# Splitting and enlarging the fill of the first four steps of a chunked scan's software pipeline

## The chip, the cores and the metric

One core of a Trainium2 chip runs the whole program. The metric is the device time of one execution in microseconds (us), as the median of several runs. Engines: PE is TensorE (matmul), PEld its weight loads, DVE VectorE, ACT ScalarE, POOL GpSimd, SP SyncE, which issues nearly all DMAs here. DVE, ACT, POOL and SP each work through their own instructions in the written order, and so does PE; they wait for each other by semaphores.

## The reference, cut to what matters

One layer of a hybrid block over 1024 latent tokens (and 256 context tokens), model width 1024, float32. An input projection `u = h @ w_in` feeds a bidirectional Mamba-2 scan (8 groups of 4 heads, head dimension 64, state 128, chunks of 128 tokens), an FNet-style Fourier branch and gates; both branches are merged, then a SwiGLU FFN and a final norm follow. The part that matters is the scan:

```
states   = einsum('bcsgn,bcsgj,bcsgjp->bcgjpn', bc, decay_to_end, xdt)
entering = scan(carry * dec + st)                      # over the chunks, each direction
cb       = einsum('bclgn,bcsgn->bcgls', cc, bc)
y_diag   = einsum('bcgjls,bcsgjp->bclgjp', cb * lmat, xdt)
y_off    = einsum('bclgn,bcgjpn,bclgj->bclgjp', cc, entering, exp(a_cum))
y        = (y_diag + y_off + xs * d_skip) * silu(z)    # then a grouped RMSNorm
```

`z` and the Fourier branch's input are column blocks of the same projection `u`; they need nothing of the scan.

## The kernel before, in words

Every projection is done in float32 by three matmuls per product: weights and activations are each split into a rounded high part and the rest, and `mm3` (lines 203 to 205) multiplies high by high, high by low, low by high into one PSUM tile.

The scan stage loops over 64 steps (`nticks`), group by group, 8 chunks of 128 tokens in each group. Step n writes, in this order: `y_b` and `y_b2` of chunk n-1; `y_a` of chunk n; the DMAs for chunk n+1 (`y_load`, whose tile `abc` has two buffers); one or two state products of the next group (`state_b`); `y_c` of chunk n-4; and then some **fill**. A Python generator `fill_stream` hands out the fill one unit at a time, and `run_fill(k)` writes units until k have been written in all. So the fill is matmul work without ties to the scan, put between the scan's short dependent products so that PE has something to do.

By names: `cb` (line 908), `yo` (910 and 911), `yd` (943), `st` (881 and 882) and `ytr` (968) are the scan's own products on PE. Their followers are `cp` (917), `G` (920), `cd` (924), `dg` (925), `y` (929), `yz` (951 and 952), the state update `S` (891) and the state weights `xwf` (873) on DVE; the eight `abc` activations (915), their Exp (918) and squares and scales (953, 961) on ACT; and `xd` (932 to 935) on POOL. `cb`, `yo`, `yd` and `st` have one PSUM buffer each.

A fill unit is one output tile of 128 tokens by 256 columns: eight times `mm3`, 24 matmuls, into a PSUM tile `fill` of three buffers (`tm_units`). Eight units share one pair of weight tiles, which two ACT casts `whi` (198) and two POOL subtractions `wlo` (199) split. Units are of two kinds. A **z unit** is turned into silu(z) by an activation (802) and a DVE step (803) into a tile `zs`, of which there are 12 buffers; `y_b2` of the same group and chunk (line 952) is the last reader and sets the buffer free. A **u unit** is copied by ACT to `ust` (807, two buffers) and stored by a DMA (808); it needs no `zs` buffer. In the stream, units 0 to 15 are z units (groups 0 and 1), 16 to 23 u units, 24 to 39 z, 40 to 47 u, 48 to 63 z, 64 to 71 u, 72 to 79 z, 80 to 87 u and 88 to 95 z. Then 20 gate units follow, in the last steps and behind the loop.

The order written here is not yet the order on the engines. Pools and a list scheduler of the tile layer place each instruction when its operands and buffers are free by that scheduler's own model; a unit written before its `zs` buffer is free stands later on PE.

Of the kernel before, what the change touches and what calls it, by code (L numbers as in the profile page):

```python
# [20 lines left out]
NT = L // P  # L21
# [114 lines left out]
def build(nc, tc, h, o, hook=None, stop=None):  # L136
    es = ExitStack()
    with es:
        _build(nc, tc, h, o, hook, stop, es)


def _build(nc, tc, h, o, hook, stop, es):
# [638 lines left out]
    NPRE = 96 + 4 * sum(GSCHED)  # L781
    RT = 1
    ZSB, FOFF = 12, 4
# [212 lines left out]
    def run_fill(n):  # L996
        while nfill[0] < n:
            nfill[0] += 1
            try:
                next(fill)  # L1000
            except StopIteration:
                return
# [11 lines left out]
    nticks = NG * NT  # L1014
    groups[0].y_load(0)
    for n in range(nticks + LAG + 1):
        g, c = divmod(n, NT)
        if n < nticks:
            if c == 0 and g + 1 < NG:
                groups[g + 1] = Group(g + 1)  # L1020
                groups[g + 1].load_states()
                groups[g + 1].state_a(0)
        if n >= 1 and n - 1 < nticks:
            groups[(n - 1) // NT].y_b((n - 1) % NT)
            groups[(n - 1) // NT].y_b2((n - 1) % NT)
        if n < nticks:
            groups[g].y_a(c)
            if n + 1 < nticks:
                groups[(n + 1) // NT].y_load((n + 1) % NT)
            if g + 1 < NG:  # L1030
                for i in ((c,) if c < 7 else (7, 8)):
                    if i + 1 < 9:
                        groups[g + 1].state_a(i + 1)
                    groups[g + 1].state_b(i)
        if n >= LAG and n - LAG < nticks:
            groups[(n - LAG) // NT].y_c((n - LAG) % NT)
        if n < nticks - NT:
            run_fill(8 + FOFF + ((NPRE - 8 - FOFF) * (n + 1)) // (nticks - NT))
        else:
            run_fill(NPRE + int(RT * (n - 55)))  # L1040
    run_fill(10 ** 6)
# [667 lines left out]
```

## Time and profile before

| | |
|---|---|
| median of 3 runs | 2231.84 us (2231.05 to 2234.35) |
| the profiled execution's own time | 2232.41 us |
| its span, first to last instruction | 2230.6 us |
| mean granted clock of TensorE | 0.994 |
| PE busy in the span | 2157.4 us, 97% |
| stage of the z and u units (612.2 to 1091.0) | 478.8 us, PE busy 462.0 |
| gate units behind it (1091.0 to 1165.0) | 74.0 us, PE busy 73.5 |

The profile lists busy time by engine, what ended each idle time, and the chain that ended last; the trace gives the same for any stretch or tile.

### The profile page before, as it was taken

To read this page: it belongs to the slowest core of one execution; us is meant where nothing else is said; L and a number is where in the kernel's file an instruction comes from. 1 tells how busy PE (TensorE), PEld (TensorE's weight loads), DVE (VectorE), ACT (ScalarE), POOL (GpSimd) and SP (SyncE) were. 2 spreads that over 40 slices of the span, in tenths; PEclk is the share of its full clock that TensorE was granted. 3 is DMA by queue.
4 is the path that set the end of the run, shared out by engine and by line. 5 is a ranking of instruction groups with operands and counts; after the bars stand their busy time and mean duration, and the time that the engine had idled before them with its cause. 6 is when DMAs were issued, how large, how long until landed. Compare 5 with 4: busy or idle time off the path is not lost.

```text
span 2230.6 us, 32729 instructions
## 1 busy us (share of the span) xinstructions
PE 2157.4 (97%) x11560; PEld 1805.8 (81%) x11560; DVE 1628.0 (73%) x2795; ACT 996.0 (45%) x2093; POOL 701.7 (31%) x581
## 2 busy tenths in 40 slices
PE   6999999999999999999999999999899999999997
PEld 1778888887798999999889887877687888878876
DVE  5888888998758777877726657946987667774577
ACT  4444444445436667666743222224532333234443
POOL 1532111010125555555521221111243333332222
PEclk9999999999999999999999999999999999999999
DMA  8212223342454555555454556752476244457765
GB/s 285 77 62 95 76 89 129 126 131 99 149 172 151 175 159 173 175 167 175 151 174 177 178 172 226 246 174 81 155 267 238 86 141 145 144 201 232 235 206 179
DMA packets 167388, 360.80 MB, mean 162 GB/s; under 512 B 17580, under 2 KB 57260, under 8 KB 166584
## 3 DMA queue, kind: packets, MB, share of 16 engines
q1 hardware_dynamic: 167224, 358.71, 47.9%
q8 instruction: 91, 1.49, 0.3%
q14 instruction: 73, 0.60, 0.1%
HBM read 267.86 MB, written 90.78 MB: 161 GB/s over the span
## 4 chain that ended last, share of the span: by engine, by line
PE 74%; DVE 10%; DMA 7%; ACT 4%; issue 3%; POOL 1%; SPq 0%; DVEq 0%; POOLq 0%; ACTq 0%
PE mm L496 16%; PE dm L210 8%; PE fp L204 6%; PE fp L205 6%; PE fp L203 5%; DMA abc<-s_a 3%; PE mm L498 3%; PE spq L210 2%; PE fq L204 2%; PE fq L205 2%; ACT abc L915 2%; PE fq L203 2%; PE fill L210 2%; PE fill L203 2%; PE fill L204 2%
## 5 line engine op out<-in xcount | busy, mean ns | idle before, releaser
L199 POOL TENSOR_TENSOR wlo<-wraw,whi 128x1024 fp32r<-128x1024 f32 x80 | 198.2, 2481 | 581.3 <-ACT whi L198 515.2
L198 ACT CAST whi<-wraw 128x1024 fp32r<-128x1024 f32 x123 | 127.8, 1044 | 218.0 <-PE dm L210 79.3
L203 PE MATMUL fill<-whi,hhi 128*128 128x256 f32 x768 | 222.3, 290 | 0.6 <-ACT whi L198 0.4
L433 DVE SCALAR_TENSOR_TENSOR cv<-pad,vecs,cv 128x1282 f32<-128x1282 f32 (+1 forms) x128 | 211.1, 1679 | 9.4 <-ACT cv L430 8.8
L204 PE MATMUL fill<-wlo,hhi 128*128 128x256 f32 x768 | 216.0, 281 | 0.2 <-POOL wlo L199 0.2
L205 PE MATMUL fill<-whi,hlo 128*128 128x256 f32 x768 | 216.0, 282 | 0.0
L915 ACT ACTIVATE abc<-abc,a_all 128x128 f32<-128x128 f32 x512 | 157.7, 389 | 90.7 <-DMA abc<-s_a 86.7
L205 PE MATMUL fp<-m,opl 128*128 128x512 f32 x452 | 179.7, 398 | 4.3 <-DVE opl L1389 4.1
L203 PE MATMUL fp<-m,oph 128*128 128x512 f32 x452 | 179.7, 398 | 2.1 <-ACT m L1432 0.9
L204 PE MATMUL fp<-m,oph 128*128 128x512 f32 x452 | 179.8, 398 | 1.8 <-DVE m L1433 1.7
L496 PE MATMUL mm<-tq,whi 128*128 128x512 f32 x480 | 155.9, 405 | 2.3 <-ACT whi L198 2.3
L203 PEld LDWEIGHTS fill<-whi,hhi 128*128 128x128 f32 x768 | 144.1, 188 | 3.0 <-ACT whi L198 0.5
L204 PEld LDWEIGHTS fill<-wlo,hhi 128*128 128x128 f32 x768 | 144.6, 188 | 1.4 <-POOL wlo L199 0.6
L205 PEld LDWEIGHTS fill<-whi,hlo 128*128 128x128 f32 x768 | 144.3, 188 | 0.5
L496 PE MATMUL mm<-hhi,whi 128*128 128x512 f32 x320 | 127.5, 399 | 3.4 <-DVE pad L572 3.4
L496 PE MATMUL mm<-hlo,whi 128*128 128x512 f32 x320 | 127.6, 399 | 0.0
L496 PE MATMUL mm<-hhi,wlo 128*128 128x512 f32 x320 | 127.3, 399 | 0.0
L917 DVE COPY_PREDICATED abc<-misc,abc 128x512 f32<-128x512 int32 x64 | 52.0, 813 | 83.4 <-ACT abc L915 83.3
L496 PEld LDWEIGHTS mm<-tq,whi 128*128 128x128 f32 x480 | 91.2, 192 | 24.1 <-ACT whi L198 3.3
L205 PEld LDWEIGHTS fp<-m,opl 128*128 128x128 f32 x452 | 85.2, 189 | 26.5 <-DVE opl L1389 5.6
L891 DVE SCALAR_TENSOR_TENSOR S<-S,ead,st 128x64 f32<-128x64 f32 x512 | 104.8, 272 | 0.0
L203 PEld LDWEIGHTS fp<-m,oph 128*128 128x128 f32 x452 | 85.3, 189 | 24.0 <-ACT m L1432 1.3
(412 smaller groups left out, 5888.7 us busy)
## 6 DMA issues: line engine op xcount, KB each, us to landing
abc<-s_a SPq DMA_DIRECT2D x64, 512.0 KB
fraw<-in_wfi SPq DMA_DIRECT2D x44, 512.0 KB
wraw<-in_wxbc SPq DMA_DIRECT2D x32, 512.0 KB
dx<-in_wada SPq DMA_DIRECT2D x32, 512.0 KB
wraw<-in_wzf SPq DMA_DIRECT2D x24, 512.0 KB
gt<-s_gate SPq DMA_DIRECT2D x24, 512.0 KB
fi<-in_wfo SPq DMA_DIRECT2D x22, 512.0 KB
s_cw<-fo SPq DMA_DIRECT2D x44, 256.0 KB
```

Source lines behind the costliest of these rows:

```text
L198: nc.scalar.copy(out=hi[:, :cols], in_=raw[:, :cols])
L199: (eng or nc.gpsimd).tensor_tensor(out=lo[:, :cols], in0=raw[:, :cols], in1=hi[:, :cols].bitcast(F32), op=ALU.subtract)
L203: nc.tensor.matmul(ps, lhsT=a[0], rhs=b[0], start=start, stop=False)
L204: nc.tensor.matmul(ps, lhsT=a[0], rhs=b[1], start=False, stop=False)
L205: nc.tensor.matmul(ps, lhsT=a[1], rhs=b[0], start=False, stop=stop)
L210: nc.tensor.matmul(ps, lhsT=a[i], rhs=b[j], start=start and (i, j) == (0, 0), stop=stop and (i, j) == (1, 0))
L433: nc.vector.scalar_tensor_tensor(out=v[:, :n], in0=pd[:, t:t + n], scalar=cwh[:, 5 * b + t:5 * b + t + 1], in1=v[:, :n], op0=ALU.mult, op1 ...
L496: nc.tensor.matmul(ps, lhsT=lhs[x], rhs=b[i][y], start=i == 0 and (x, y) == (0, 0), stop=i == 3 and (x, y) == (1, 0))
L498: nc.tensor.matmul(cps, lhsT=lhs[x], rhs=(hc_hi, hc_lo)[y][c0 + i], start=first and i == 0 and (x, y) == (0, 0), stop=last and i == 3 and ...
L891: nc.vector.scalar_tensor_tensor(out=sn[:, hd_], in0=S[-1][:, hd_], scalar=decp[:, i, d, 4 * g + j:4 * g + j + 1], in1=sv_[:, hd_], op0=AL ...
L915: nc.scalar.activation(out=abc[:, d, j, :], in_=abc[:, d, j, :], func=AF.Identity, scale=-1.0, bias=a_all[:, c, hd:hd + 1])
L917: nc.vector.copy_predicated(out=E, mask=tri_b.bitcast(mybir.dt.int32)[:, None, :].to_broadcast([P, HPG, P]), data=abc[:, 1])
```

## The change

The fill of steps 0 to 3 is written in two parts. A first part stands ahead of `y_a`, up to 10, 13, 16 and 19 units in all; the second stands where it did, up to 12, 15 and 18. From step 3 on, the count rises evenly from 22 to 96 at step 55. Before, it rose evenly from 13 at step 0 to 96 at step 55. So after step 0 there is one unit less, after step 1 as many, after step 2 two more, after steps 3 to 5 four more, and the lead runs out towards step 55. No instruction is added or taken away.

```
         if n >= 1 and n - 1 < nticks:
             groups[(n - 1) // NT].y_b((n - 1) % NT)
             groups[(n - 1) // NT].y_b2((n - 1) % NT)
+        if n < 4:
+            run_fill(10 + 3 * n)
         if n < nticks:
             groups[g].y_a(c)
...
         if n < nticks - NT:
-            run_fill(8 + FOFF + ((NPRE - 8 - FOFF) * (n + 1)) // (nticks - NT))
+            run_fill(12 + 3 * n if n < 3 else 21 + ((NPRE - 21) * (n - 2)) // (nticks - NT - 3))
```

What the scheduler makes of it on the engines is shown at three places. The first is PE between the `yo` products of chunk 4 and `yd` of chunk 3, with the first three of the 24 matmuls of unit 16. Before:

```order
L908 MATMUL cb<-cT,bT 128x128
L910 MATMUL yo<-S_5151,cT 128x256
L911 MATMUL yo<-S_5111,cT 128x256
L881 MATMUL st<-xwf,bh 128x256
L882 MATMUL st<-xwb,bh 128x256
L203 MATMUL fill<-whi,hhi_190 128x256
```

and with the change:

```order
L910 MATMUL yo<-S_5151,cT 128x256
L911 MATMUL yo<-S_5111,cT 128x256
L203 MATMUL fill<-whi,hhi_190 128x256
L204 MATMUL fill<-wlo,hhi_190 128x256
L205 MATMUL fill<-whi,hlo_198 128x256
```

All 24 matmuls of unit 16 now stand ahead of the state product `st`, where they stood behind it.

The second place is ACT in the steps that follow, where the u units are copied out. Before, copies of u units alternate with the scan's activations:

```order
L807 COPY ust<-fill 128x256
L971 ACTIVATE yst<-ytr,vecs 128x128 x2
L953 ACTIVATE xd,ssq<-yz 128x256
L918 ACTIVATE abc<-abc 128x512
L807 COPY ust<-fill 128x256 x2
L953 ACTIVATE xd,ssq<-yz 128x256
L971 ACTIVATE yst<-ytr,vecs 128x128 x2
```

and with the change:

```order
L807 COPY ust<-fill 128x256
L915 ACTIVATE abc<-abc,a_all 128x128 x8
L961 ACTIVATE yz<-yz,grs 128x256 x2
L807 COPY ust<-fill 128x256
L918 ACTIVATE abc<-abc 128x512
L807 COPY ust<-fill 128x256 x4
L971 ACTIVATE yst<-ytr,vecs 128x128 x2
```

Four copies now stand in a row: on PE, units 17 to 22 are written with only one `st` between them, ahead of `yd` of chunk 4. Before, `yd` of chunk 4 stood behind unit 18.

The third place is PE around chunks 12 and 13 with the change, from the last matmul of unit 33 to what stands right ahead of unit 34:

```order
L205 MATMUL fill<-whi,hlo_205 128x256
L908 MATMUL cb<-cT,bT 128x128
L943 MATMUL yd<-xh,G 128x64 x4
L910 MATMUL yo<-S_6265,cT 128x256
L911 MATMUL yo<-S_5897,cT 128x256
L968 MATMUL ytr<-misc,yz 128x128 x2
L881 MATMUL st<-xwf,bh 128x256
L882 MATMUL st<-xwb,bh 128x256
L908 MATMUL cb<-cT,bT 128x128
L943 MATMUL yd<-xh,G 128x64 x4
L910 MATMUL yo<-S_6359,cT 128x256
L911 MATMUL yo<-S_5741,cT 128x256
```

Two `yd` and two `cb` stand here with no fill between them; before, there were one and a half units between the same two `yd`. From here to the start of unit 41, PE has seven units (34 to 40) for eight `yd` (of chunks 12 to 19; the first one shown is chunk 12's), and then units 41 to 45 in a row. Such a stretch comes again between units 62 and 65, with two units (63 and 64) for four steps.

## Rows read from the trace of the kernel before

**Rows 1.** The page: the span and the busy time of PE.
```profile
span 2230.6 us, 32729 instructions
PE 2157.4 (97%) x11560; PEld 1805.8 (81%) x11560; DVE 1628.0 (73%) x2795; ACT 996.0 (45%) x2093; POOL 701.7 (31%) x581
```

**Rows 2.** Stretches: start:end, length, busy us of each engine, clock, DMA share, GB/s.
```profile
650.00:660.00 10.00, 10.00 (x82) 9.79 (x81) 5.83 (x24) 0.39 (x1) 1.85 (x3) 1.00 0.08 23
660.00:670.00 10.00, 7.55 (x49) 6.38 (x48) 6.54 (x25) 3.08 (x9) 2.05 (x4) 1.00 0.49 160
670.00:680.00 10.00, 8.48 (x52) 7.27 (x52) 7.69 (x22) 6.08 (x16) 6.41 (x9) 1.00 0.35 107
680.00:690.00 10.00, 8.25 (x58) 7.25 (x57) 10.00 (x28) 4.55 (x16) 7.89 (x8) 1.00 0.50 166
...
612.20:1091.00 478.80, 461.98 (x3488) 439.32 (x3487) 353.39 (x1119) 304.93 (x928) 246.94 (x290) 1.00 0.52 166
```

**Rows 3.** Timeline of PE: the starts of units 0 and 1, then two `yd`.
```profile
612.24 0.28 PE L203 MATMUL fill<-whi,hhi 128*128 128x256 f32 x1
615.04 0.28 PE L203 MATMUL fill<-whi,hhi 128*128 128x256 f32 x1
...
704.14 1.00 PE L943 MATMUL yd<-xh,G 128*128 128x64 f32 x8
710.01 1.00 PE L943 MATMUL yd<-xh,G 128*128 128x64 f32 x8
```

**Rows 4.** Timeline of PE in the first hole: start, length, instruction, [idle before, released by].
```profile
666.42 0.49 PE L908 MATMUL cb<-cT,bT 128*128 128x128 f32 x2 [1.07 <-DVE cd L924]
668.29 0.70 PE L911 MATMUL yo<-S,cT 128*128 128x256 f32 x2 [1.38 <-DVE S L891]
...
671.68 0.70 PE L910 MATMUL yo<-S,cT 128*128 128x256 f32 x2 [0.78 <-DVE y L929]
...
673.55 0.70 PE L881 MATMUL st<-xwf,bh 128*128 128x256 f32 x2 [0.74 <-ACT S L887]
...
674.52 1.00 PE L943 MATMUL yd<-xh,G 128*128 128x64 f32 x8
```

**Rows 5.** Timeline of PE, chunk 4's second `yo`, the wait behind it, `yd` of chunk 3.
```profile
681.56 0.59 PE L911 MATMUL yo<-S,cT 128*128 128x256 f32 x2
683.87 0.67 PE L881 MATMUL st<-xwf,bh 128*128 128x256 f32 x2 [1.71 <-DVE S L891]
...
687.61 1.00 PE L943 MATMUL yd<-xh,G 128*128 128x64 f32 x8
```

**Rows 6.** Timeline of DVE, the same time.
```profile
682.11 1.61 DVE L891 SCALAR_TENSOR_TENSOR S<-S,ead,st 128x64 f32<-128x64 f32 x8
683.64 0.41 DVE L803 SCALAR_TENSOR_TENSOR zs<-zs,fill 128x256 f32<-128x256 f32 x1
```

**Rows 7.** A group of ACT: line, operation, count, busy us, mean ns, idle us before.
```profile
L915 ACT ACTIVATE abc<-abc,a_all 128x128 f32<-128x128 f32 x512 | 157.7, 389 | 90.7 <-DMA abc<-s_a 86.7
```

**Rows 8.** One stretch of DVE from 700 to 1050: a count of chunks; the stretch's busy times.
```profile
L920 DVE TENSOR_TENSOR G<-abc,cb 128x512 f32<-128x512 f32 x45 | 30.6, 680 | 0.6 <-PE cb L908 0.5
...
700.00:1050.00 350.00, 339.50 (x2575) 324.03 (x2574) 264.56 (x837) 234.40 (x728) 186.47 (x222) 1.00 0.53 168
```

**Rows 9.** From `yd` of chunk 18 to that of chunk 20: the stretch, PE's wait, DVE, POOL.
```profile
801.98:818.62 16.64, 14.78 (x114) 14.05 (x113) 15.31 (x42) 11.11 (x34) 12.98 (x13) 1.00 0.60 188
...
812.08 0.67 PE L881 MATMUL st<-xwf,bh 128*128 128x256 f32 x2 [1.86 <-issue]
...
804.44 2.13 DVE L952 TENSOR_TENSOR yz<-yz,zs 128x256 f32<-128x256 f32 x1
807.09 1.99 DVE L925 SCALAR_TENSOR_TENSOR dg<-dt_all,dg,rows 128x4 f32<-128x4 f32 x1
...
803.89 2.39 POOL L199 TENSOR_TENSOR wlo<-wraw,whi 128x1024 fp32r<-128x1024 f32 x1
```

**Rows 10.** Timeline of PE: waits of its later steps.
```profile
934.33 0.67 PE L881 MATMUL st<-xwf,bh 128*128 128x256 f32 x2 [1.61 <-issue]
...
965.08 0.67 PE L881 MATMUL st<-xwf,bh 128*128 128x256 f32 x2 [1.31 <-DVE S L891]
...
1026.02 0.67 PE L881 MATMUL st<-xwf,bh 128*128 128x256 f32 x2 [1.52 <-DVE S L891]
```

More of the change, by code (lines that the diff above doesn't have):

```diff
@@ L1025, in _build @@
             groups[(n - 1) // NT].y_b2((n - 1) % NT)
+        if n < 4:
+            run_fill(10 + 3 * n)
         if n < nticks:
@@ L1037, in _build @@
         if n < nticks - NT:
-            run_fill(8 + FOFF + ((NPRE - 8 - FOFF) * (n + 1)) // (nticks - NT))
+            run_fill(12 + 3 * n if n < 3 else 21 + ((NPRE - 21) * (n - 2)) // (nticks - NT - 3))
         else:
```

## The prediction

> **What bounds the kernel now.** The page comes first: PE is busy for 2157.4 of 2230.6 us [rows 1], so only idle time of PE can be won. The stretches show where it lies. In the stage of the z and u units PE is busy for 461.98 of 478.80 us [rows 2], so 16.8 us are idle, and no placing of the fill can win more. A good third of it stands in one hole: between 660 and 690 PE is busy for 7.55, 8.48 and 8.25 us of 10 each [rows 2], 5.7 us idle. The rest lies mostly in short waits for DVE's state update: 1.86 us at 812, 1.61 at 934, 1.31 at 965, 1.52 at 1026 [rows 9, 10].
>
> The timeline gives the price of a step. A unit takes 615.04 - 612.24 = 2.80 us [rows 3]. The two `yd` at 704.14 and 710.01 have one unit between them [rows 3], so a step costs PE 5.87 us with one unit, 3.07 without. The next engine is DVE: 264.56 us of busy time from 700 to 1050, in which it makes 45 `G`, one a chunk [rows 8], so 5.88 us a step. **With one unit a step, PE and DVE need the same**; the mean of 1.5 units (7.3 us) keeps PE the bound. Where fewer stand, DVE becomes the bound.
>
> **The change part by part.** No matmul, copy or DMA is added or removed; the terms are the waits that go and come.
>
> *The first hole stays, 0.* Its four waits are for DVE's `cd`, DVE's `S`, DVE's `y` and ACT's copy of a state: 1.07, 1.38, 0.78 and 0.74 us, ended by `yd` of chunk 1 at 674.52 [rows 4]. The changed kernel has the same order there: unit 14, then these products, then unit 15. The reason is the buffers: unit 12 is the thirteenth `zs` tile of twelve, and with three PSUM buffers unit 15 can't begin until `y_b2` of chunk 0 has freed one. Units written earlier don't get past that. Moving `cb` of chunk 0 back by one unit costs nothing: what comes of it is used only behind unit 11, three units later.
>
> *Unit 16 ahead of `st`, -1.2 us.* PE now waits 1.71 us for `S` behind chunk 4's `yo` [rows 5]; unit 16 (2.80 us) covers this, and `st` is then no longer early. But unit 16 needs the PSUM buffer of unit 13, whose last reader `zs` ran from 683.64, behind the 1.61 us of `S` that began at 682.11 [rows 6]. The changed order puts it ahead of `S`, so it ends about 683.64 + 0.41 - 1.61 = 682.4; PE was free at about 681.56 + 0.59 = 682.15 and waits 0.3 to 0.5 us. Of 1.71 I take 1.2 as won; bounds 0 and 1.7.
>
> *Units 17 to 22 in a row, 0.* PE stays busy. Each copy to `ust` must come within 2.80 us, and four of them stand on ACT behind the eight `abc` activations (8 x 0.389 = 3.1 us at most, the mean by the count [rows 7]) of chunk 7. Three PSUM buffers give PE 8.4 us of lead, more than 3.1 plus an Exp and two scales. Bounds: 0, and one such set in full, 3.1. The stores are issued one after another by SP with the load of `abc` for chunk 7 ahead of them, so that load isn't held. DVE has less to do meanwhile, but behind it there are 11 units for eight steps (1.4 each), so it isn't the bound there.
>
> *The stretch from unit 34 to unit 41, +1.1 us net.* The lead runs into the `zs` limit: units 24 to 39 are 16 z units, and one buffer comes free per step. PE's own work is eight steps of 3.07, seven units of 2.80 and about 1.9 us of a ninth step's products: 24.6 + 19.6 + 1.9 = 46.1 us. DVE's eight steps take 8 x 5.88 = 47.0. So if DVE never waited, PE would idle 0.9 us. In the same steps before, DVE was busy for 15.31 of 16.64 us, 92% [rows 9]; at that share the stretch takes 47.0 / 0.92 = 51.1, and PE idles 5.0. I take 3.0, the middle, since that row has waits of its own kind in it. The wait of 1.86 us [rows 9] stood in these steps and is replaced: net +1.1. The high bound is the first hole's pace: from 674.52 to 687.61 [rows 4, 5] two steps with one unit each took 6.55 apiece, 0.68 more than PE's 5.87; eight such steps give 5.4, and with a load of `abc` late as there (ACT waited 86.7 us in all for them [rows 7]) I allow 8.
>
> Part of that share is lost to POOL. While a `wlo` ran for 2.39 us from 803.89, DVE's `yz` took 2.13 us, and a `dg` of 4 columns 1.99 behind it [rows 9], where a `zs` of the size of `yz` takes 0.41 [rows 6]: about 3.5 us lost to a pair of `wlo`. The changed order keeps one such pair inside this stretch. [...]
>
> *The stretch from unit 62 to unit 65, +0.6 us net.* Units 62 to 64 and about 4.5 steps: 3 x 2.80 + 4.5 x 3.07 = 22.2 us for PE, against 4 x 5.88 = 23.5 for DVE: 1.3 idle at best, and 23.5 / 0.92 - 22.2 = 3.3 at 92%. I take 2.2; 1.61 us [rows 10] stood in those steps before. Bounds 0 and 5.
>
> *All later waits, 0.* From chunk 39 on the two orders differ by one unit or less, and 1.31 and 1.52 us [rows 10] stay; they could go or double. Behind the scan the gate units keep PE busy, so what the stage gains or loses passes to the end in full.
>
> Sum: -1.2 + 1.1 + 0.6 = **+0.5 us**. The profiled execution's own time of 2232.41 us (1.8 above its span) would be 2232.9, and it stands 0.6 above the median of 2231.84, so the median becomes **2232.3 us**. About 0.2% (4.5 us) is what a measurement of this kernel can tell from no change.
>
> **The rivals.**
>
> *The hole fills.* If DVE or ACT come earlier in the first steps than I read, or the fill gets between the hole's products, 4.0 us of waits [rows 4] go with the 1.71, and the later stretches keep at their best (0.9 + 1.3 against 1.86 + 1.61): -4.0 - 1.7 - 1.3 = -7 us, 2225. A milder form leaves the hole and wins only the late state waits, -1.7 - 1.3 - 2.8 = -5.8, 2226. For it: the hole is the largest idle piece. Against it: the order there is unchanged, and the limit is in buffers. By the stretches' weight loads the hole is larger: 9.79 of 10 us in a full window, then 6.38, 7.27 and 7.25 [rows 2], 8.5 us short where PE's busy time says 5.7. [...] Chance of the rival: 0.22.
>
> *DVE becomes the bound where the lead meets the `zs` limit* (slower). Place: units 34 to 41 and 62 to 65. If DVE, waiting in turn for POOL and ACT, runs at the first hole's pace or below, the prices are 8 and 5 us; less the 3.5 replaced and with nothing won at unit 16 that is +9.5, 2241. It decides above 0.2% when DVE is busy under about 88% there (47.0 / 0.88 - 46.1 = 7.3 and 23.5 / 0.88 - 22.2 = 4.5; less 3.5 and 1.2, +7; the border of 4.5 us lies at 91%). For it: nearly equal needs, no slack on either side. Against: such steps already stood singly before with 92%. Chance: 0.28.
>
> *Four copies in a row hold PE* (a part of the former's side): +3.1, 2235, inside 0.2% alone. 0.05 of the middle case.
>
> **How the numbers follow.** The forecast, the stage moving by under 4.5 us either way, has 0.5; faster by over 0.2% 0.22; slower 0.28. The range reaches from the milder gain to the full loss less a little, 2225.5 to 2240, and leaves about 2 in 10 outside. The forecast's own range is 2227.5 to 2236.5.
>
> **What would show it.** Right: the same four waits between about 665 and 674; no 1.7 us wait ahead of unit 16; PE without a gap through units 17 to 22; new waits of PE, for `S`, `y` or the `zs` steps, in the steps of chunks 12 to 20 and 32 to 37, 3 and 2 us in sum; DVE there above 90% busy. PE's idle time of the stage near 17 us again. Wrong: the first hole shorter by microseconds, or either stretch idle by over 6 us, or a wait for an `ust` copy.

## The result, and the profile after

The changed kernel takes **2246.95 us** (2243.65 to 2249.09, 4 runs) against 2231.45 us (2227.6 to 2234.35, 4 runs) for the kernel before: ratio 1.0072, 95% interval 1.0059 to 1.0085, some 16 us slower. The prediction was 2232.3 us with a range up to 2240; the measured time lies above it.

The page of the kernel after, span and PE's busy time; a longer span, and PE busy for 9.1 us longer with as many instructions [rows 1].

```profile
span 2247.3 us, 32740 instructions
...
PE 2166.5 (96%) x11560; PEld 1812.6 (81%) x11560; DVE 1623.9 (72%) x2795; ACT 995.6 (44%) x2093; POOL 702.4 (31%) x581
```

Stretches of the kernel after (start:end, length, busy us of PE, PEld, DVE, ACT, POOL, granted clock, DMA share, GB/s), the first four as in [rows 2]; the last is the whole stage from the first fill unit to the last gate unit.

```profile
650.00:660.00 10.00, 9.99 (x82) 9.71 (x82) 6.33 (x25) 2.81 (x9) 1.78 (x3) 1.00 0.12 41
660.00:670.00 10.00, 6.50 (x39) 5.57 (x38) 5.64 (x24) 3.08 (x9) 1.84 (x3) 0.89 0.42 137
670.00:680.00 10.00, 9.22 (x32) 7.13 (x32) 6.82 (x18) 4.38 (x14) 5.90 (x8) 0.60 0.19 61
680.00:690.00 10.00, 10.00 (x79) 9.69 (x79) 9.52 (x26) 6.55 (x18) 7.64 (x7) 1.00 0.58 182
...
610.80:1182.60 571.80, 545.63 (x3859) 508.16 (x3858) 380.81 (x1197) 345.87 (x1047) 277.39 (x323) 0.98 0.50 160
```

The same stage of the kernel before, in five pieces, cut where `yd` of chunks 12, 20, 25 and 50 begins, and whole:

```profile
612.20:755.28 143.08, 136.54 (x1030) 129.36 (x1029) 97.92 (x308) 76.39 (x221) 63.61 (x73) 1.00 0.50 163
755.28:818.62 63.34, 60.25 (x454) 57.01 (x453) 51.98 (x161) 43.35 (x134) 38.81 (x44) 1.00 0.55 176
818.62:857.88 39.26, 38.88 (x298) 37.23 (x297) 28.71 (x91) 26.53 (x84) 21.74 (x26) 1.00 0.60 189
857.88:1049.40 191.52, 184.93 (x1402) 176.53 (x1402) 142.72 (x456) 128.75 (x402) 99.42 (x121) 1.00 0.52 164
1049.40:1164.50 115.10, 114.88 (x682) 100.29 (x681) 61.60 (x182) 70.58 (x211) 53.04 (x60) 1.00 0.47 157
...
612.20:1164.50 552.30, 535.48 (x3857) 500.42 (x3855) 382.92 (x1195) 345.60 (x1047) 276.63 (x323) 1.00 0.51 166
```

And the kernel after, cut at the same chunks:

```profile
610.80:765.55 154.75, 148.54 (x1103) 141.04 (x1102) 98.51 (x312) 79.65 (x225) 69.57 (x76) 0.97 0.49 158
765.55:835.03 69.48, 63.25 (x456) 59.08 (x457) 53.59 (x168) 48.51 (x152) 36.31 (x46) 0.98 0.51 163
835.03:869.80 34.77, 34.77 (x269) 33.48 (x268) 23.65 (x77) 20.43 (x62) 15.98 (x18) 1.00 0.49 157
869.80:1068.20 198.40, 184.67 (x1355) 174.12 (x1354) 143.48 (x462) 126.72 (x397) 104.08 (x126) 0.98 0.54 164
1068.20:1182.60 114.40, 114.40 (x683) 100.43 (x683) 61.58 (x183) 70.56 (x211) 51.45 (x58) 1.00 0.46 154
```

The stage is 571.80 - 552.30 = 19.5 us longer; what lies ahead and behind is 1.4 us shorter each. In these two profiled executions the 19.5 split in two halves of different kinds. **Idle** time of PE went from 16.8 to 26.2 us, 9.35 more. **Busy** time went from 535.48 to 545.63, 10.15 more, for the same products: there the granted clock fell.

Three windows of 5 us show it. In windows of 1 us the clock at these places and at the first hole is 1.00 or 0.50, and between the two (0.84 to 0.99) only where it turns; the values below stand between because a window of 5 us holds both.

```profile
800.00:805.00 5.00, 4.71 (x19) 3.87 (x19) 4.30 (x9) 4.55 (x18) 4.66 (x7) 0.66 0.66 210
...
980.00:985.00 5.00, 4.04 (x16) 3.51 (x17) 2.68 (x10) 5.00 (x13) 3.95 (x3) 0.68 0.64 151
...
1055.00:1060.00 5.00, 3.87 (x15) 3.52 (x16) 3.74 (x10) 3.24 (x10) 3.03 (x5) 0.69 0.27 89
```

Time that a low clock costs is worked out as length times (1 - clock), summed over all windows of 5 us in the stage below 0.99. For the kernel after it is 10.2 us: 5.1 from 665 to 680, and 1.7 each at 800, 980 and 1055. That is the 10.15 us by which PE was busier. The kernel before has no such window in its stage.

Over all executions the clock's part is smaller than in this pair. The mean granted clock was 0.990 in the change's four (span times (1 - clock) makes 23 us) and 0.992 to 0.993 in the five sets of executions of the kernel before (16 to 18.5 us; the profiled execution has 0.994). By this estimate some 4 to 7 of the 16 us are clock, and the larger part is idle time.

PE's timeline in the first hole of the kernel after, beside [rows 4]:

```profile
666.79 0.49 PE L908 MATMUL cb<-cT,bT 128*128 128x128 f32 x2 [2.12 <-DVE cd L924]
668.66 1.22 PE L911 MATMUL yo<-S,cT 128*128 128x256 f32 x2 [1.38 <-DVE S L891]
...
671.38 1.06 PE L910 MATMUL yo<-S,cT 128*128 128x256 f32 x2
672.23 1.06 PE L911 MATMUL yo<-S,cT 128*128 128x256 f32 x2
674.08 1.22 PE L910 MATMUL yo<-S,cT 128*128 128x256 f32 x2 [0.78 <-DVE y L929]
```

A pair of `yo` products starts 0.85 us behind the one before it (672.23 - 671.38), and the row reads 1.06 us where [rows 5] have 0.59: the clock is 0.50 in each window of 1 us from 668 to 678, and 1.00 in those from 660 to 667 and from 679 to 690. What stood ahead of each of the four falls is a wait: 2.12 and 1.38 us here, 1.86 at 796.8, 2.54 at 978.4, 2.39 at 1053.7. But 2.70 us at 939.4 was followed by no fall, and the kernel before waited 1.86 us ahead of 812.1 [rows 9] without one.

**Excess** is the measure for the rest: the length of a piece less 3.07 us a step and 2.80 us a unit, the prices of [rows 3]. Before, chunks 13 to 20 had 12 units: 63.34 - 8 x 3.07 - 12 x 2.80 = 5.2 us. (The cuts shown are rounded, so the last digit can differ by 0.1.)

| piece | before | after | difference |
|---|---|---|---|
| first unit to `yd` of chunk 12 (31 units; 34) | 16.3 | 19.7 | +3.4 |
| chunks 13 to 20 (12; 12 units) | 5.2 | 11.3 | +6.1 |
| chunks 21 to 25 (8; 7) | 1.6 | -0.2 | -1.8 |
| chunks 26 to 50 (37; 35) | 11.2 | 23.6 | +12.4 |

Behind chunk 50 the difference is -0.6. The biggest loss stands where the forecast had 0.6 and 0. The excess holds the low clock too: of the change's, 5.1 us in the first piece, 1.7 in the second and 3.4 in the last.

### The profile page after: what moved, and what is told of

It reads as the page before. It is cut to its first block, busy times and chain, and to the rows that moved or that the text cites. A ratio compares the mean times of both kernels' runs of the same rounds, so it can differ in the third digit from the quotient of the medians.

```text
span 2247.3 us, 32740 instructions
## 1 busy us (share of the span) xinstructions
PE 2166.5 (96%) x11560; PEld 1812.6 (81%) x11560; DVE 1623.9 (72%) x2795; ACT 995.6 (44%) x2093; POOL 702.4 (31%) x581
## 4 chain that ended last, share of the span: by engine, by line
PE 72%; DVE 10%; DMA 7%; ACT 4%; issue 3%; POOL 2%; SPq 0%; POOLq 0%; DVEq 0%; ACTq 0%
PE mm L496 16%; PE dm L210 8%; PE fp L204 5%; PE fp L205 5%; PE fp L203 5%; DMA abc<-s_a 4%; PE mm L498 3%; PE spq L210 2%; PE fq L204 2%; PE fq L205 2%; PE fq L203 2%; PE fill L210 2%; PE fill L203 2%; PE fill L204 2%; PE fill L205 2%
```

## The experiments

All ratios are to the kernel before, timed on the same chip. "Lead" means the units that the change has done, at a given chunk, beyond the kernel before: 4 at chunk 4, 3 at chunks 12 and 20, 1 or none from chunk 32 on.

**1 and 2. Which of the two edited lines.** The front part alone, then the later numbers alone:

```
# run 1, on the kernel before
+        if n < 4:
+            run_fill(min(10 + 3 * n, 8 + FOFF + ((NPRE - 8 - FOFF) * (n + 1)) // (nticks - NT)))
# run 2, on the changed kernel
-        if n < 4:
-            run_fill(10 + 3 * n)
```

> The kernel before with the front part of the change, but the end of a step asks for no more than before, so the units lead nowhere. The lead theory (the three to four units that the change brings forward leave later steps with one unit or none, where TensorE waits for the chain of the scan): nothing to lose, 2227 to 2236 us. The rival, that writing the fill in front of the first products is what costs (later cd, another order of the loads of abc): 2243 to 2250 us as in the changed kernel.

> The changed kernel without its front part: each step's end asks for the change's numbers, so the lead is the same from chunk 5 on. Lead theory: 2243 to 2250 us, as slow as the change. The rival of the front part: 2227 to 2236 us. If both have a share, it lies between, near 2240.

Run 1: 2232.25 us, ratio 1.0004 (0.999 to 1.0018). Run 2: 2251.19, ratio 1.0087 (1.0068 to 1.0105). Where the fill is written costs nothing that can be measured; the lead costs all.

**3 and 4. With more `zs` buffers; with the lead given back at once.**

```
# run 3
-    ZSB, FOFF = 12, 4
+    ZSB, FOFF = 16, 4
# run 4: one unit a step from step 4 on, until the numbers of before are reached
-            run_fill(12 + 3 * n if n < 3 else 21 + ((NPRE - 21) * (n - 2)) // (nticks - NT - 3))
+            run_fill(12 + 3 * n if n < 4 else max(18 + n, 8 + FOFF + ((NPRE - 8 - FOFF) * (n + 1)) // (nticks - NT)))
```

> The changed kernel with 16 buffers of zs instead of 12; the order then has units 13 to 18 between the products of the first hole, and chunks 12 to 20 get 1 to 2 units a step instead of none to two and then six. If the limit of the zs buffers makes the loss: the first hole (4 us) goes, and the 6.2 us that chunks 13 to 20 lost come back, 2232 to 2238 us. If any lead costs, with buffers or not (one unit a step is too few for DVE and ACT): 2240 to 2247 us.

> The changed kernel, whose step ends ask from step 4 on for one unit a step until the numbers of the kernel before are reached, in step 11: by the order the lead is gone by chunk 9, and from there on the order is that of before. If the loss is made where the lead meets the z units (17 of 19.4 us behind chunk 12 by the timeline): 2230 to 2237 us. If each one-unit step costs wherever it stands, the six of them that now stand in chunks 5 to 9 cost what those of chunks 13 to 19 did, and the later losses go: 2236 to 2241. If the burst at the start is the loss, 2243 to 2250 us.

Run 3: 2234.57 us, ratio 1.002 (1.0007 to 1.0033). What the lead costs with 16 buffers is read against run 13 below. Run 4: 2229.95, ratio 0.9997 (0.9985 to 1.0009). Run 4 has the burst and, between 660 and 675, clocks of 0.92, 0.50 and 0.56 as the change has; with the lead gone by chunk 9 the whole costs nothing that can be measured. Steps with one unit or less cost nothing there: chunks 5 to 7 have 2.6 units and take 15.4 us, less than 3 x 3.07 + 2.6 x 2.80 = 16.5.

**5 to 8. The first hole filled, and a third buffer of `abc`.** The eight u units of the first set need no `zs`, so they can be brought right behind units 0 to 7:

```
         yield from tm_units(0)
+        yield from tm_units(NG)
...
-            if g in (1, 3, 5, 6):
+            if g in (3, 5, 6):
# runs 7 and 8 also
-            abc = pb.tile([P, 2, HPG, P], F32, name="abc", bufs=2)
+            abc = pb.tile([P, 2, HPG, P], F32, name="abc", bufs=3)
```

> The changed kernel, but the fill brings the eight u units of the first set right behind units 0 to 7 and the z units of group 1 behind them. Units 13 to 18 then stand in the first hole; behind chunk 5 the numbers of units are those of the change. If the lead costs where it meets the z units of group 2 and later: only the start's loss and hole go (3 us lost, 4 us of waits), the later losses of 16 us stay, 2236 to 2243 us. If the loss behind chunk 12 comes from the disturbed start: 2226 to 2232 us.

> The kernel before with the same order of the fill (u units of the first set behind units 0 to 7) and its own numbers: units 13 to 18 fill the first hole, the chunks 4 to 8 get about 0.6 units a step, from chunk 9 on all is as before. If the hole is fillable when its units are not bound to the zs buffers and steps with half a unit pass there: 4.0 us of waits and the 1.7 go, 2223 to 2228 us. If the lead is paid back in the steps with half a unit at the same rate: 2229 to 2235 us.

> As the run with the change and the u units first, with a third buffer of abc; chunks 12 to 19 get the same units a step as there. If the idle time in those steps comes from the chain of abc (buffer free, load, eight scalings on ACT, copy on DVE, products): ACT's waits for the load and DVE's waits for ACT go there, the residual of chunks 13 to 20 falls from about 9 to under 4 us, and the time is 5 to 12 us below that run's. If DVE's own work is the limit there: within 2 us of that run.

> The kernel before with the u units first and a third buffer of abc. If late loads of abc make the waits that are left in the kernel before (some 10 us behind chunk 12): 3 to 6 us below the run with two buffers. If they are DVE's: within 2 us of it.

Run 5 (change): 2242.36 us, ratio 1.0056 (1.0038 to 1.0075). Run 6 (before): **2223.14**, ratio 0.9974 (0.9963 to 0.9985), faster than both kernels. Run 7 (change, 3 `abc`): 2242.19, ratio 1.0056 (1.0041 to 1.0071). Run 8 (before, 3 `abc`): 2226.06, ratio 0.9983 (0.9971 to 0.9996). The hole of run 6, against [rows 2]:

```profile
660.00:670.00 10.00, 10.00 (x80) 9.73 (x79) 5.89 (x16) 6.50 (x17) 6.35 (x5) 1.00 0.58 189
670.00:680.00 10.00, 10.00 (x75) 9.58 (x75) 8.92 (x24) 4.15 (x14) 5.32 (x8) 1.00 0.44 147
...
609.20:1155.40 546.20, 534.25 (x3859) 501.13 (x3858) 384.12 (x1196) 345.36 (x1047) 277.85 (x323) 1.00 0.52 167
```

So the hole can be filled: that is worth 0.0026 of the time without the lead (5.8 us) and 0.0016 with it (1.0072 - 1.0056). The lead costs 0.0082 with the hole filled (1.0056 - 0.9974), about as much as without. Run 5 has no profile that can be read by pieces; runs 7 and 8 stand for the pair below. The theory of run 7, that loads of `abc` start the waits, rested on this chain of the changed kernel ahead of its wait at 796.8, rows of PE, ACT and DVE:

```profile
796.41 0.39 PE L908 MATMUL cb<-cT,bT 128*128 128x128 f32 x2
798.66 0.70 PE L910 MATMUL yo<-S,cT 128*128 128x256 f32 x2 [1.86 <-DVE y L929]
...
794.32 0.99 ACT L915 ACTIVATE abc<-abc,a_all 128x128 f32<-128x128 f32 x3 [1.03 <-DMA abc<-s_a]
...
797.31 0.73 DVE L917 COPY_PREDICATED abc<-misc,abc 128x512 f32<-128x512 int32 x1 [2.93 <-ACT abc L915]
797.93 0.68 DVE L929 TENSOR_TENSOR y<-yo,ead 128x512 f32<-128x512 f32 x1
```

The load is late, ACT's scalings are late, DVE waits 2.93 us, and `y`, whose `yo` was done at 795.5, stands behind it in DVE's order; PE's next `yo` needs the buffer that this `y` sets free. Run 7 took the buffer limit away, and its waits in the same steps are these:

```profile
789.87 0.70 PE L910 MATMUL yo<-S,cT 128*128 128x256 f32 x2 [1.89 <-DVE y L929]
...
804.79 0.67 PE L881 MATMUL st<-xwf,bh 128*128 128x256 f32 x2 [2.75 <-DVE S L891]
...
799.72 2.57 DVE L952 TENSOR_TENSOR yz<-yz,zs 128x256 f32<-128x256 f32 x1
```

They are no smaller, the second now behind a `yz` of 2.57 us. The theory of the `abc` buffers falls.

**9 and 10. Less work for DVE.** Four instructions a direction become one:

```
-                    for j in range(HPG):
-                        hd_ = slice(j * HD, j * HD + HD)
-                        nc.vector.scalar_tensor_tensor(out=sn[:, hd_], in0=S[-1][:, hd_], scalar=decp[:, i, d, 4 * g + j:4 * g + j + 1],
-                                                       in1=sv_[:, hd_], op0=ALU.mult, op1=ALU.add)
+                    nc.vector.scalar_tensor_tensor(out=sn, in0=S[-1], scalar=decp[:, i, d, 4 * g:4 * g + 1],
+                                                   in1=sv_, op0=ALU.mult, op1=ALU.add)
```

> Changes the computation: the state update takes one decay factor for the four heads of a group, so one DVE instruction of 256 columns stands for four of 64 (about 0.82 us a step for 1.62, an estimate from the S and zs rows). The changed kernel so cut; the units' numbers a step stay but for chunks 3 and 4. To be read against the next run, the kernel before cut alike. If DVE's work bounds the steps with one unit (5.88 us against TensorE's 5.87): the loss behind chunk 12 goes, this run is within 6 us of that one. If not DVE's work but the buffers or loads bound them: 12 to 18 us above it.

> Changes the computation: as the run before this one, on the kernel before. By either theory a little below the kernel before, since part of its waits are for S: 2220 to 2229 us.

Run 9: 2244.61 us, ratio 1.0067 (1.0052 to 1.0082). Run 10: 2233.75, ratio 1.0025 (1.0016 to 1.0035). The lead costs 0.0042 here, about 9 us, between the two expectations. Run 10 is slower than the kernel before, which neither theory expected: its DVE has 48.6 us less to do in the stage (334.30 for 382.92), but the scheduler's order moves with the durations, and its trace has waits that were not there (2.21 us for `G` at 735.7, 2.42 for `whi` at 885.3). Why was not followed. So the smaller difference comes from a slower partner: run 9 itself (1.0067) is about as slow as the change (1.0072).

**11 and 12. The clock.** Unit 12 does its first three (six) accumulation steps twice:

```
+            for k in (range(3) if nfill[0] == 13 else ()):
...
+                mm3(ps, (h_hi[k][:, tsl], h_lo[k][:, tsl]), (hi[:, wsl], lo[:, wsl]), k == 0, k == 2)
```

> The changed kernel, in which unit 12, ahead of the first hole, does the first three of its eight accumulation steps twice (the first pass is overwritten): 9 more products, 1.05 us at 0.117 us each. If the lower granted clock behind the first hole comes from the idle time in it: the hole shrinks by about 1 us, the stretch 665 to 680 stays at the upper level, 2240 to 2245 us. If the clock falls for another reason, or costs nothing: 2246 to 2250 us.

> As the run before this one with six steps done twice: 18 more products, 2.1 us, and the burst of units moves from chunk 4 to chunk 5. Clock from idle time: 665 to 680 at the upper level, 2239 to 2245 us in spite of the added work. Otherwise 2247 to 2252 us.

Run 11: 2247.73 us, ratio 1.0079 (1.0066 to 1.0092). Run 12: 2250.48, ratio 1.0097 (1.0084 to 1.011). No time was won, so both lie where the second theory of each put them. In run 11 the clock does stay up from 660 to 690, although waits of 1.48, 1.38, 0.78, 0.79, 1.21 and 1.22 us stand there, but falls at 770, 810, 940 and 1050 instead (8.5 us in all). That shorter waits spare the clock is not shown.

**13 to 16. Which part of the lead.** The partner of run 3; a lead that is never given back; a lead only up to chunk 22; a lead only from chunk 20.

```
# run 13, on the kernel before
-    ZSB, FOFF = 12, 4
+    ZSB, FOFF = 16, 4
# run 14, on run 3 (and 4 more behind the 56th step)
-            run_fill(12 + 3 * n if n < 3 else 21 + ((NPRE - 21) * (n - 2)) // (nticks - NT - 3))
+            run_fill(12 + 3 * n if n < 3 else 4 + 8 + FOFF + ((NPRE - 8 - FOFF) * (n + 1)) // (nticks - NT))
# run 15, on the change: from step 21 on
+            max(n + 26, 8 + FOFF + ((NPRE - 8 - FOFF) * (n + 1)) // (nticks - NT))
# run 16, on the kernel before: from step 17 on
+            max(min(42 + 2 * (n - 18), 21 + ((NPRE - 21) * (n - 2)) // (nticks - NT - 3)), 8 + FOFF + ((NPRE - 8 - FOFF) * (n + 1)) // (nticks - NT))
```

> The kernel before with 16 buffers of zs; units 13 to 18 fill the first hole as in the run with the change and 16 zs, and no unit leads behind chunk 8. If the zs limit is the whole cost of a lead: within 4 us of that run with the lead (ratio 1.002), so 2230 to 2236 us. If steps thinned by the lead cost without the limit too: like the kernel before with the u units first, 2220 to 2227 us, and the lead still costs some 11 us with 16 buffers.

> The change with 16 buffers of zs and a lead of four units that is kept to the end of the scan (each later step asks for the numbers of the kernel before plus four): by the order every step has its 1.5 units and none is thinned. If giving the lead back in thinned steps is the cost: as fast as the kernel before with 16 zs, 2220 to 2228 us. If units and weights that stand elsewhere against the scan cost as such: 2231 to 2238 us, as with the change and 16 zs.

> The changed kernel, whose step ends from step 21 on ask for one unit a step until the numbers of before are reached (chunk 25); from there on the order of before. If the loss is local, each stretch paying for itself: the start and chunks 12 to 20 stay (2.7 and 6 us), the 16 us behind shrink to the five thinned steps, 2236 to 2243 us. If one place, chunks 12 to 20, makes it all: 2243 to 2250.

> The kernel before up to chunk 18, then the change's numbers: three units are brought forward in chunk 20, and the rest of the order is that of the change. If the loss is local: the 9 to 10 us that the change lost behind chunk 25 come, and nothing ahead of it, 2236 to 2243 us. If chunks 12 to 20 make it all: 2228 to 2234.

Run 13: **2221.81 us**, ratio 0.9969 (0.9957 to 0.998), the fastest measured; against it the lead of run 3 still costs 0.0051, some 11 us, with 16 buffers. Run 14: 2231.58, ratio 1.0015 (1.0003 to 1.0026), 0.0046 above run 13 and in the range of its second theory. Run 15: 2237.21, ratio 1.0039 (1.0023 to 1.0054). Run 16: 2239.28, ratio 1.0048 (1.0032 to 1.0065). The loss is local: up to chunk 22 it is 0.0039, from chunk 20 on 0.0048, and the sum is that of the lead alone in run 2.

Where it goes is read by pieces. Pieces of two runs, chunks 13 to 20 of run 3 (11 units), then chunks 26 to 50 of run 9 (35 units):

```profile
757.33:814.45 57.12, 56.73 (x431) 54.22 (x430) 45.65 (x145) 40.73 (x129) 30.05 (x38) 1.00 0.51 163
```

```profile
862.34:1053.19 190.85, 183.39 (x1354) 172.37 (x1353) 126.15 (x306) 125.67 (x392) 101.78 (x123) 0.99 0.51 168
```

The first leaves PE idle for 0.39 us of 57.12. All pairs by excess, worked out as above from one profiled execution each; in brackets what of it the low clock makes:

| pair | chunks 13 to 20, no lead / lead | chunks 21 to 25 | chunks 26 to 50 |
|---|---|---|---|
| before / change | 5.2 / 11.3 (1.7) | 1.6 / -0.2 | 11.2 / 23.6 (3.4) |
| u first, 3 `abc` (runs 8 / 7) | 3.7 / 12.1 (1.7) | 0.9 / 0.7 | 13.2 (1.7) / 22.5 (5.1) |
| 16 `zs` (runs 13 / 3) | 2.2 / **1.8** | 1.7 / **7.0** (1.7) | 10.4 / 20.3 (3.4) |
| less DVE work (runs 10 / 9) | 3.1 / 10.1 (1.7) | 3.2 / 0.5 | 14.8 (3.4) / **16.1** (1.7) |
| 16 `zs`, lead kept (runs 13 / 14) | 2.2 / **1.6** | 1.7 / 3.2 | 10.4 / **6.8** |
| lead up to chunk 22 (before / run 15) | 5.2 / 13.8 (5.1) | 1.6 / 0.3 | 11.2 / **10.5** |
| lead from chunk 20 (before / run 16) | 5.2 / **5.6** | 1.6 / 1.4 | 11.2 / 21.9 (3.4) |

One execution is a rough measure: among the traces with DVE's full work, chunks 26 to 50 read 10.2 to 13.2 us in the seven without a lead there, and 19.3 to 23.6 in the seven where one is given back.

In **chunks 13 to 20** the loss goes with four more `zs` buffers and stays with less DVE work: the buffer limit makes the order uneven there (by the order no unit in chunks 13 and 19, six in a row in chunk 20). But with 16 buffers most of it comes back in chunks 21 to 25, 7.0 us for 1.7. The piece of run 3 with its seven units:

```profile
814.45:856.40 41.95, 38.12 (x274) 35.92 (x273) 30.46 (x97) 26.31 (x82) 22.44 (x28) 0.96 0.55 174
```

In **chunks 26 to 50** the loss stays with 16 buffers, shrinks to 1.3 us with less DVE work (3.0 without the low clock in both), and goes where the lead is kept. A third `abc` helps in neither stretch. That DVE's work makes the loss there is not shown, though: behind chunk 50, up to the last gate unit, run 9 is 5.0 us longer than run 10, where the change is no longer than the kernel before. Run 9, then run 10:

```profile
1053.19:1172.30 119.11, 116.81 (x682) 100.38 (x680) 61.24 (x143) 72.29 (x217) 53.80 (x60) 1.00 0.43 147
```

```profile
1050.40:1164.50 114.10, 114.09 (x682) 100.09 (x680) 57.05 (x136) 69.51 (x209) 52.19 (x58) 1.00 0.45 151
```

From chunk 26 to the end of the stage, without the low clock, the lead then costs 3.0 + 5.0 = 8.0 us with less DVE work and 12.4 - 0.6 - 3.4 = 8.4 with all of it. The whole stage says the same. Runs 3, 9 and 10 (that of run 13 follows below):

```profile
607.70:1166.60 558.90, 539.58 (x3857) 505.77 (x3855) 384.66 (x1199) 345.01 (x1047) 277.44 (x323) 0.99 0.50 164
```

```profile
609.90:1172.30 562.40, 543.89 (x3857) 503.96 (x3855) 345.29 (x813) 346.12 (x1047) 279.07 (x323) 0.99 0.49 162
```

```profile
608.80:1164.50 555.70, 539.16 (x3857) 504.81 (x3855) 334.30 (x813) 345.65 (x1047) 275.33 (x323) 0.99 0.51 164
```

The low clock makes 5.1, 3.4 and 5.1 us of these. Without it the lead costs the stage 19.5 - 10.2 = 9.3 us in the change, 558.9 - 545.3 - 5.1 = 8.5 with 16 buffers and 562.4 - 555.7 + 1.7 = 8.4 with less DVE work. Neither measure takes the loss away; each moves it. It is gone only where the lead is kept (run 14, inside the stage) or given back by chunk 9 (run 4). Of the waits in chunks 26 to 50 of the change, DVE's `S`, `y` and `G` ended 5.9 us, ACT's `whi` and `yst` 4.1, and 2.7 us ended with nothing that the profile names. What makes the steps lose stays open.

**Run 14** shows what a kept lead then costs. Its stage and that of run 13, whole:

```profile
609.90:1151.00 541.10, 534.64 (x3857) 500.91 (x3855) 384.64 (x1197) 346.49 (x1045) 280.50 (x323) 1.00 0.50 164
```

```profile
609.50:1154.80 545.30, 534.19 (x3857) 500.93 (x3855) 382.65 (x1198) 346.25 (x1047) 277.07 (x323) 1.00 0.52 168
```

The stage of run 14 is 4.2 us shorter, and PE is idle in it for 6.5 us only. Behind it, rows of SP's queue and of PE in run 14:

```profile
1151.39 0.81 SPq L822 DMA_DIRECT2D s_gate<-gt  x2
...
1153.73 0.91 SPq L1100 DMA_DIRECT2D U<-s_u  x2
...
1159.15 3.03 PE L1105 MATMUL sab<-tf,U 128*128 128x128 f32 x13 [7.97 <-DMA U<-s_u]
```

and in run 13 (its lines have lower numbers):

```profile
1146.29 0.92 SPq L1098 DMA_DIRECT2D U<-s_u  x2
...
1155.75 1.49 PE L1103 MATMUL sab<-tf,U 128*128 128x128 f32 x11 [0.99 <-ACT gt L821]
```

The last gate units covered the load of `U`; done earlier, they leave PE waiting 7.97 us, and the clock falls (3.4 us by windows).

**17. A kept lead of one unit.** Run 13 with the change's front part and one unit more at each step's end (and one more behind the 56th step):

```
-            run_fill(8 + FOFF + ((NPRE - 8 - FOFF) * (n + 1)) // (nticks - NT))
+            run_fill(12 + 3 * n if n < 2 else 1 + 8 + FOFF + ((NPRE - 8 - FOFF) * (n + 1)) // (nticks - NT))
```

> The kernel before with 16 buffers of zs and a lead of one unit (the change's front part, each step's end asks for the numbers of before plus one) that is kept to the end. In the run with four kept units the stage itself took 541.1 us against 545.3 without a lead, and then the first transposes behind it waited 7.97 us for U, whose load starts when the scan ends. If that is all that a kept lead costs: with one unit the load (5.4 us there) is covered again, the wait at the first transposes is under 2 us, and the time 2218 to 2223 us. If a lead costs inside the scan even where it is kept: 2224 to 2230 us.

2231.47 us, ratio 1.0011 (1.0002 to 1.0021): above both expectations, and 9.7 us above run 13. The wait for `U` was 2.49 us, the stage 546.9 us against 545.3, what lies behind 1.8 us longer; the other 3.9 us of the 7.3 by which its profiled execution is longer lie ahead of the first unit, where single executions of these kernels differ by as much (606.9 to 613.4 us). What makes a kept unit cost that much stays open, and with it whether a kept lead is free.

## Why the prediction was wrong

- *The first hole stays, 0.* The waits did: 2.12 + 1.38 + 0.78 = 4.28 us against 3.97 [rows 4]. `cb` waits twice as long: PE reached it 0.7 us earlier (664.66 for 665.35), and `cd`, behind a load of `abc` in DVE's order, came 0.4 us later (the load took 4.6 us from its issue to ACT's start for 3.8). Whether that comes from moving `cb` of chunk 0 back is not shown. What failed is the term of 0: waits of nearly the same length cost more, by the clock (5.1 us from 665 to 680). From the first unit to `yd` of chunk 1 it now takes 677.65 - 610.78 = 66.9 us instead of 674.52 - 612.24 = 62.3 [rows 3, 4].
- *Unit 16 ahead of `st`, -1.2.* Right, and a little more: the wait of 1.71 us [rows 5] is gone, and chunk 3's step, 7.60 us before, takes 5.64. It made up for a part of the former only.
- *Units 17 to 22 in a row, 0.* Right: chunk 4's step of 19.82 us is 3.07 + 6 x 2.80 within 0.1. The rival of four `ust` copies didn't come.
- *The stretch from unit 34 to unit 41, +1.1.* The idle time came out above the 3.0 forecast and below the bound of 8: waits of 0.29, 1.79, 1.86, 0.29 and 1.82 us, 6.1 in all, in place of 1.86. But DVE's own work was not the price. DVE was busy for 53.59 of 69.48 us there, 77%, far from the 92% that the sum went by, and less DVE work changed little (10.1 for 11.3 us). PE's waits did end with DVE's `y` and `S`; what made DVE late is not shown. An even order, with 16 buffers, took the loss out of these chunks, though not out of the next five. And 1.7 us of low clock came on top.
- *The stretch from unit 62 to unit 65, +0.6, and "all later waits, 0".* This is the step that failed most: +12.4 us in chunks 26 to 50, 6.1 of them in the stretch itself (chunks 32 to 37) and 5.9 from chunk 38 on (3.4 by the low clock at 980 and 1055). The prediction had "the two orders differ by one unit or less", so the waits of 1.31 and 1.52 us were to stay; instead waits of 2.54 and 2.39 us came. Chunks 32 to 37 hold nine units in both kernels, before and after:

```profile
904.00:949.50 45.50, 43.89 (x337) 42.17 (x337) 36.53 (x111) 30.44 (x95) 25.48 (x30) 1.00 0.55 168
```

```profile
913.50:965.10 51.60, 46.68 (x346) 43.53 (x345) 36.65 (x122) 31.94 (x100) 27.12 (x33) 1.00 0.53 162
```

The excess is 45.50 - 6 x 3.07 - 9 x 2.80 = 1.9 us before and 8.0 after. By the order the change has the nine as 1, 1, 1, 1, 2 and 3 a step, the kernel before as 1, 2, 1, 0.5, 2.5 and 2. So a count of units with a balance of PE and DVE does not give the price: DVE was busy for 36.65 of 51.60 us, 71%, and single steps with one unit cost nothing in either kernel (5.87 us each at chunks 42 and 50, as in [rows 3]). The traces show the loss in and behind a row of four thin steps, in runs 2 and 16 at the same place as in the change; in run 4 a row of three cost nothing, and through which engine the loss comes is open.
- *The sum.* **The clock's term was missing**: 10.2 of 19.5 us in the profiled pair, some 4 to 7 of 16 over all executions. The rows ahead of the prediction show 1.00 throughout the stage, and the sum took idle time to cost only itself.
- *The rivals.* "DVE becomes the bound where the lead meets the `zs` limit" came nearest: it gave +9.5 us, and idle time rose by 9.35. That the two numbers agree is in part luck. Its two places were right, and DVE was busy there for under its 88% (77% and 71%), with PE idle for 6.2 and 4.9 us against its prices of 8 and 5. But it had nothing for the chunks from 38 on, nor for the clock, and that DVE is the bound is not shown: with less DVE work the lead costs the stage as much. "The hole fills" can be had: runs 6 and 13 do it, with units that meet no limit. What that is worth in run 6, 0.26% or 5.8 us, lies nearer to the 5.7 us that PE's busy time gives for the hole than to the 8.5 us of the weight loads: as the price of this hole the measurement speaks for the busy time.

More buffers took the loss out of one stretch only. With 16 `zs` buffers and the lead, chunks 13 to 20 have 1.8 us of excess for 11.3, but 7.0 us then stand in chunks 21 to 25; a third `abc` leaves 12.1 us in chunks 13 to 20, and in chunks 26 to 50 the two leave 20.3 and 22.5 us of 23.6.

## What to carry to other kernels

Independent work placed early has to be missed later: look at how it is spread over every step behind the place, not only where a buffer limit shows, since thin steps in a row lost time in the change (8.0 us of excess for 1.9 in chunks 32 to 37) where single ones lost none (5.87 us each). A remedy that mends one stretch is to be judged by the whole stage, because the loss can move. To fill a hole, change which work stands near it (here units that need no limited buffer), so that the numbers behind it stay as they were. And price a wait of the matmul engine at its length and what the granted clock may lose behind it (here 1.7 us behind each of three waits of 1.86 to 2.54 us, and nothing behind one of 2.70).

## What was not expected of the hardware

Falls of the granted clock from 1.00 to 0.50, in or shortly behind waits of 1.38 to 2.54 us, made the products behind them take nearly twice as long: the row of a pair of `yo` went from 0.59 to 1.06 us, with about 1.7 us lost at each of three places and 5.1 at the first hole of the change. In the profiled executions that were read for it, the stage's busy time of PE less the time that the low clock costs is 533 to 537 us, whatever the order; only run 9 has 540.5. Which wait brings a fall was not settled: 2.70 us passed without one, and 1.86 us did and didn't.
